# An encoder layer in fp32: input projection in seven block products, values in 512-wide products, chains in a new order

## The chip, the cores and the metric

The kernel runs on one core of a Trainium2 chip. The metric is the device time of one launch in microseconds (us), the median of the runs. A profile is one execution, recorded by the hardware profiler.

## The reference, cut to what matters

One encoder layer with shared weights runs on two groups of tokens: 256 of a prompt and 1024 of a sample, 1280 in all, width 1024. All is fp32.

```python
h = rmsnorm(x, g_mix_pre)
z = h @ w_in                      # 1024 x 9216
rq, rk, rv, rg, pin, mq, gl = split(z)    # six of 1024 columns, gl of 3072
gates  = sigmoid(gl)
y_ret  = retention_branch(rq, rk, rv, rg) @ w_ret_out   # rotary on q and k, chunks, both directions; silu(rg)
y_pool = pool_branch(pin) @ w_pool_out                  # moving means of width 2, 4, 8, 16
y_mem  = memory_branch(mq, mem) @ w_mem_out             # kv = rmsnorm(mem) @ w_mem_kv; softmax attention
merged = gates[0] * y_ret + gates[1] * y_pool + gates[2] * y_mem
x = x + rmsnorm(merged @ w_o, g_mix_post)
x = x + rmsnorm(conv_ffn(rmsnorm(x), w_up, conv_w, conv_b, w_down), g_ffn_post)
```

## The kernel before, in words

**Numbers.** A number is held as a high and a low part in a rounded fp32 format. `hilo` (L138) makes them: ScalarE copies to the high part (L140), VectorE subtracts for the low part (L141). A product is three matmuls, `mm3` (L147): high by high, high by low, low by high (L148 to L150), added up in one PSUM bank.

**Tiles.** The normed tokens lie transposed in SBUF as `hT`, eight tiles of 128 features by 1280 tokens, high and low. A *unit* is a 128 by 1024 tile of weights. For a feature-major unit, `fm_groups` (L481) makes 128 output features for three groups of tokens (512, 512, 256), with the weights as the stationary operand: 24 matmuls a group. For values, tokens are stationary and 256 columns of weights move, 24 matmuls for each 128 tokens (L624 to L630).

**Weights.** The class `Weights` (L59) takes units from one list `srcs` in the order of their use. A unit is loaded by SP into one of two raw tiles (L71), split by ScalarE (L87) and VectorE (L88) into one of four pairs of tiles, and taken by `take` (L96). The load of the unit after next is issued when a split is written.

**Order.** The program's order is written out by hand, and each engine runs its own instructions in that order. `tick` (L271) is called after each group of tokens (in the rotary units after each two groups): it splits a unit, issues one step of the weight sums, and takes one step of every chain in `bg`. A *chain* is a generator that does the work of one branch between `yield`s, beside the projections. The stages are:

1. The memory stage (L436 to L478): the statistics of mem and x, `hT`, the decay tables (`decay_tables` L398, with the decay matrix `dtab` and its load of `rel`), the memory's keys (8 units) and its values (4 heads, 256 columns each, L460 to L477), beside the chains `mem_stats`, `x_stats` and `decay_tables`.
2. Memory queries `mq` (8 units, VectorE copies them out of PSUM to SBUF, L619), then retention values (L622 to L635), beside `mem_chain` (L502): scores, softmax, products with the memory's values, stores of `om`.
3. Four times two pool units (`pool_unit`, L709) and a rotary query unit pair (`rotary_unit`, L726), then four key pairs, beside `pool_chain` (L645).
4. Retention gates `rg` (8 units, L826 to L834), beside `state_chain` (L750), which builds the states of the retention.
5. Branch gates (24 units, `gate_unit` L956). Beside the first of them runs `ret_chain` (L837): for each of 20 jobs (4 heads, 5 chunks) the scores, the products with values and with states, the norm, transposes and the store of `yr` (L934). It takes two steps a job and two steps a unit, after the groups of 512.
6. From 1347 us: products of the branches with their output weights, the output projection, the up projection, the convolution, the down projection.

**The up projection** (L1341 to L1555) makes two units (one gate, one value) of 1024 sample tokens with seven block products where eight would be direct. Four blocks of `h2` and three of their sums are kept (`hterm`), and two sums of weights a pair are made ahead, in DRAM, by DMAs: `sums` (L243) issues for each pair two plain DMAs on SP's queue (L251, L252) and four that accumulate on POOL's queue (L254 to L260), one step a tick, from the start of stage 2 on.

**Banks.** PSUM has eight banks of 512 columns: four for projections (`mmb`) and four for chains (`chb`).

Of the kernel before, what the change touches and what calls it, by code (L numbers as in the profile page):

```python
# [24 lines left out]
H = 4  # L25
# [13 lines left out]
PCOLS = PW - 2 * PAD  # L39
SLOT = 2 * T  # L40
# [18 lines left out]
class Weights:  # L59
# [8 lines left out]
    def load(self):  # L68
        if self.n_load < self.load_limit and self.n_load < self.n_split + self.RAW:
            t = self.pool.tile([P, 1024], F32, tag="wr", name="wr", bufs=self.RAW)  # L70
            self.nc.sync.dma_start(out=t, in_=self.srcs[self.n_load])  # L71
            self.raw[self.n_load] = t
            self.n_load += 1
# [22 lines left out]
    def take(self, n=1):  # L96
# [7 lines left out]
        return out  # L104

# [5 lines left out]
def encoder(ctx: ExitStack, tc: tile.TileContext, a: dict):  # L111
# [68 lines left out]
    w_in = a["w_in"]  # L180
    srcs = [a["w_kv"][i] for i in range(16)]
    srcs += [w_in[40 + i] for i in range(8)]
    srcs += [w_in[16 + i] for i in range(8)]
    for h in range(H):
        srcs += [w_in[32 + 2 * h], w_in[33 + 2 * h], w_in[2 * h], w_in[2 * h + 1]]
    srcs += [w_in[8 + i] for i in range(8)]
    srcs += [w_in[24 + i] for i in range(8)]
    srcs += [w_in[48 + i] for i in range(24)]
# [4 lines left out]
    s12_d = [dram.tile([P, 2, 512], F32, name=f"s12d{q}") for q in range(NF)]  # L193
    s34_d = [dram.tile([P, 2, 512], F32, name=f"s34d{q}") for q in range(NF)]
# [4 lines left out]
    for nm, q in stream:  # L199
        srcs.append({"u0": a["w_up"][q], "a2": a["w_up"][NF + q],  # L200
                     "s12": s12_d[q][:].rearrange("p a b -> p (a b)"),
                     "s34": s34_d[q][:].rearrange("p a b -> p (a b)")}[nm])
# [24 lines left out]
    vm_d = [dram.tile([P, 4, HD], F32, name=f"vm{h}") for h in range(H)]  # L227
    q_d = [dram.tile([P, NCH, 2, C], F32, name=f"qd{h}") for h in range(H)]
    k_d = [dram.tile([P, NCH, 2, C], F32, name=f"kd{h}") for h in range(H)]
    v_d = [dram.tile([P, NCH, 2, HD], F32, name=f"vd{h}") for h in range(H)]  # L230
# [12 lines left out]
    def sums():  # L243
        lag = 2

        def stage(i, q):
            u, v = (a["w_up"][n].rearrange("p (a b) -> p a b", b=512) for n in (q, NF + q))
            both = lambda x: x.unsqueeze(1).to_broadcast([P, 2, 512])
            s12, s34 = s12_d[q], s34_d[q]
            if i == 0:  # L250
                nc.sync.dma_start(out=s12[:], in_=both(v[:, 0, :]))  # L251
                nc.sync.dma_start(out=s34[:], in_=u)  # L252
            elif i == 1:
                nc.gpsimd.dma_start(out=s12[:], in_=both(v[:, 1, :]), accum_op=ALU.add)  # L254
            elif i == 2:
                nc.gpsimd.dma_start(out=s34[:, 0, :], in_=v[:, 0, :], accum_op=ALU.add)
            elif i == 3:
                nc.gpsimd.dma_start(out=s12[:, 1, :], in_=u[:, 0, :], accum_op=ALU.add)
            else:
                nc.gpsimd.dma_start(out=s34[:, 1, :], in_=s12[:, 1, :], accum_op=ALU.add)  # L260

        for n in range(NF + 4 * lag):
            for i in range(5):
                q = n - lag * i
                if 0 <= q < NF:
                    stage(i, q)
                    yield

    summing = [None]

    def tick(step=True):  # L271
        ws.tick()
        if summing[0] is not None:
            next(summing[0], None)
# [13 lines left out]
    ds = ExitStack()  # L288
    dec = ds.enter_context(tc.tile_pool(name="dec", bufs=1))
# [62 lines left out]
    def x_stats():  # L352
# [15 lines left out]
        xrb = s0.tile([P, T], F32, name="xrb")  # L368
# [27 lines left out]
    dtab = dec.tile([P, H, 2, C], F32, name="dtab")  # L396

    def decay_tables():  # L398
# [24 lines left out]
        nc.vector.tensor_scalar(out=kd, in0=kd, scalar1=HD ** -0.5, scalar2=None, op0=ALU.mult)  # L423
        yield
        rel = s0.tile([P, 2, 2 * C], F32, name="rel")
# [600 lines left out]
    for _ in summing[0]:  # L1026
        pass
# [734 lines left out]
```

## Time and profile before

| | |
|---|---|
| median of 3 runs | 2675.5 us (2675.26 to 2675.93) |
| the profiled execution's own time | 2674.43 us |
| span of the profile | 2672.7 us |
| TensorE busy | 2641.5 us, 14396 matmuls |
| VectorE, ScalarE, POOL busy | 1351.4, 919.5, 280.0 us |
| TensorE's granted clock, mean | 0.995 |

The span reaches from the first instruction to the last. A matmul's row covers its whole passage, so rows of neighbours overlap, and the busy time of TensorE says that it had work, not that it ran at its peak. Times in rows are us, and ns for the mean of one instruction. In a wait, the name behind the arrow is what ended it.

### The profile page before, as it was taken

The numbers are of one execution on the slowest core, as the hardware profiler recorded it, in microseconds if no ns is written. First come the engines' busy times: TensorE is split into PE (matmuls) and PEld (weight loads), VectorE is DVE, ScalarE is ACT, GpSimd is POOL, SyncE is SP. The second block draws the span as 40 slices with busy tenths as digits, with TensorE's granted clock in tenths as the row PEclk, the third lists the DMA queues.
The fourth block names the chain that finished last, engine by engine and source line by source line (L and its number), as shares of the span: only waits on it lengthen the run. The fifth ranks groups of instructions, "written<-read, shape, count | busy, mean of one in ns | idle before, by whom it ended". The sixth has DMA issues, their size and how long they took to land.

```text
span 2672.7 us, 36264 instructions
## 1 busy us (share of the span) xinstructions
PE 2641.5 (99%) x14396; PEld 2292.0 (86%) x14396; DVE 1351.4 (51%) x2267; ACT 919.5 (34%) x1567; POOL 280.0 (10%) x457
## 2 busy tenths in 40 slices
PE   8999999999999999999999999999999999999998
PEld 6999998888888888888888888877888888888887
DVE  5645303445445355555433453557666665664554
ACT  5433311221024332332312020565444444444443
POOL 1111221211123111111100000110000000000000
PEclk9999999999999999999999999998999999999999
DMA  7775565665477544444434353452333333354443
GB/s 263 255 197 142 142 154 158 149 170 142 123 177 215 170 155 150 142 156 147 141 133 138 107 168 97 146 185 92 113 109 116 111 111 110 116 190 148 140 159 111
DMA packets 145434, 397.57 MB, mean 149 GB/s; under 512 B 17680, under 2 KB 27792, under 8 KB 144912
## 3 DMA queue, kind: packets, MB, share of 16 engines
q1 hardware_dynamic: 100128, 267.02, 30.6%
q0 software_dynamic: 44848, 127.95, 17.6%
q8 instruction: 113, 1.85, 0.3%
q14 instruction: 57, 0.47, 0.1%
q10 hardware_dynamic: 288, 0.28, 0.0%
HBM read 303.69 MB, written 143.39 MB: 167 GB/s over the span
## 4 chain that ended last, share of the span: by engine, by line
PE 93%; issue 2%; DMA 2%; DVE 1%; ACT 1%; POOL 0%; SPq 0%; DVEq 0%; ACTq 0%; POOLq 0%
PE f L1316 15%; PE mm L149 13%; PE mm L148 13%; PE mm L150 13%; PE f L150 10%; PE f L149 10%; PE f L148 10%; PE ch L149 3%; PE ch L150 3%; PE ch L148 3%; DMA wr<-w_kv_in 0%; PE ch L559 0%; PE ch L931 0%; PE ch L769 0%; DMA x2d<-x 0%
## 5 line engine op out<-in xcount | busy, mean ns | idle before, releaser
L148 PE MATMUL mm<-b,wh 128*128 128x512 f32 (+1 forms) x1536 | 545.7, 355 | 0.0
L149 PE MATMUL mm<-b,wh 128*128 128x512 f32 (+1 forms) x1536 | 544.3, 354 | 0.0
L150 PE MATMUL mm<-b,wl 128*128 128x512 f32 (+1 forms) x1536 | 543.7, 354 | 0.0
L88 DVE TENSOR_TENSOR wl<-wr,wh 128x1024 fp32r<-128x1024 f32 x244 | 297.7, 1224 | 407.1 <-ACT wh L87 402.3
L87 ACT ACTIVATE wh<-wr 128x1024 fp32r<-128x1024 f32 x244 | 255.3, 1050 | 277.3 <-PE f L149 150.4
L150 PEld LDWEIGHTS mm<-b,wl 128*128 128x128 f32 x1536 | 290.0, 189 | 40.8
L148 PEld LDWEIGHTS mm<-b,wh 128*128 128x128 f32 x1536 | 290.4, 189 | 39.2
L149 PEld LDWEIGHTS mm<-b,wh 128*128 128x128 f32 x1536 | 290.4, 189 | 38.4
L1316 PE MATMUL f<-b,wh 128*128 128x512 f32 x880 | 274.3, 393 | 0.0
L1316 PEld LDWEIGHTS f<-b,wh 128*128 128x128 f32 x880 | 162.3, 190 | 30.7
L1316 PE MATMUL f<-b,wl 128*128 128x512 f32 x440 | 171.9, 391 | 0.0
L149 PE MATMUL f<-b,wh 128*128 128x512 f32 (+1 forms) x432 | 153.4, 355 | 0.0
L148 PE MATMUL f<-b,wh 128*128 128x512 f32 (+1 forms) x432 | 153.1, 355 | 0.0
L150 PE MATMUL f<-b,wl 128*128 128x512 f32 (+1 forms) x432 | 152.8, 354 | 0.0
L150 PE MATMUL f<-wh,gl 128*128 128x512 f32 x390 | 151.8, 389 | 0.1
L148 PE MATMUL f<-wh,gl 128*128 128x512 f32 x390 | 151.9, 389 | 0.0
L149 PE MATMUL f<-wl,gl 128*128 128x512 f32 x390 | 151.7, 389 | 0.0
L141 DVE TENSOR_TENSOR gl<-b,gl 128x640 fp32r<-128x640 f32 x78 | 64.4, 825 | 118.1 <-ACT gl L140 118.1
L964 ACT ACTIVATE gate<-mm 128x512 f32<-128x512 f32 (+1 forms) x68 | 35.5, 522 | 223.7 <-PE mm L150 133.0
L140 ACT ACTIVATE gl<-b 128x640 fp32r<-128x640 f32 x78 | 57.5, 740 | 153.9 <-PE f L150 153.9
L1316 PE MATMUL f<-hc,wh 128*128 128x512 f32 x352 | 108.9, 391 | 0.0
L148 PE MATMUL f<-h2p,wh 128*128 128x256 f32 x352 | 100.3, 285 | 3.3 <-ACT h2p L140 3.3
(343 smaller groups left out, 5293.5 us busy)
## 6 DMA issues: line engine op xcount, KB each, us to landing
wr<-w_in_in SPq DMA_DIRECT2D x72, 512.0 KB, 4.0
wr<-w_up_in SPq DMA_DIRECT2D x44, 512.0 KB, 3.6
wr<-w_down_in SPq DMA_DIRECT2D x44, 512.0 KB, 3.6
b<-fgd SPq DMA_DIRECT2D x44, 320.0 KB, 5.2
h2s<-gtd SPq DMA_DIRECT2D x48, 256.0 KB, 3.8
s12d<-w_up_in SPq DMA_DIRECT2D x22, 512.0 KB, 6.7
s34d<-w_up_in SPq DMA_DIRECT2D x22, 512.0 KB, 7.4
s12d<-w_up_in POOLq DMA_DIRECT2D x22, 512.0 KB, 7.8
```

The source lines that it names most:

```text
L87: self.nc.scalar.activation(h, r[:], AF.Copy)
L88: self.nc.vector.tensor_tensor(out=l, in0=r[:], in1=h.bitcast(F32), op=ALU.subtract)
L140: nc.scalar.activation(hi, src, AF.Copy)
L141: nc.vector.tensor_tensor(out=lo, in0=src, in1=hi.bitcast(F32), op=ALU.subtract)
L148: nc.tensor.matmul(out, ah, bh, start=first, stop=False)
L149: nc.tensor.matmul(out, ah, bl, start=False, stop=False)
L150: nc.tensor.matmul(out, al, bh, start=False, stop=last)
L964: nc.scalar.activation(y[:, 0:n], b, AF.Sigmoid)
L1316: nc.tensor.matmul(b, w[x][:, ks], hterm(nm, c, y), start=first and c == k == 0, stop=last and c == 3 and k == 2, skip_group_check=True)
```

## The change

- **Twelve pairs.** The units of `mq`, `pin` and `rg` are taken in twelve pairs. For a pair, the sample's 1024 tokens are made with seven block products (84 matmuls of 512) and the prompt's 256 tokens directly (48 of 256). Results go to DRAM (`mq_d`, `pin_d`, `g_d`), and the chains load them from there. The sums of tokens `T1` to `T4` are made by `in_terms` beside the values: xT is loaded again on ScalarE's queue, and VectorE and ScalarE scale, mix and split it.
- **Weight sums.** `sums` covers 34 pairs, twelve of the input projection ahead of the 22 of the up projection. Its first step goes to ScalarE's queue. Its steps start with the memory's values (one a tick), go on at two a tick in the values, and at one a released unit in the pairs (four a pair).
- **Values.** Both kinds are made 512 columns wide (`token_major`): four units are held for a half of the columns, and blocks of four token tiles fill four banks. ScalarE copies them out and stores them on its own queue, through two staging tiles (retention) or three (memory).
- **Order.** Memory keys; memory values; retention values; pairs; then keys beside `mem_chain` and one gate; nine gates beside `pool_chain` and `decay_matrix`; queries beside `state_chain`; gates beside `ret_chain`, which steps four times a unit, once of it in the middle of the first group; then the gates that are left. `rotary_unit` ticks after every group.
- `decay_matrix` (the load of `rel` and `dtab`) leaves the memory stage. In `ret_chain` the next job's split stands before the transposes and the output. Several pools wait tile by tile for the space that they reuse.

```diff
+    quads = [(k, i, w_in[o + 2 * i], w_in[o + 2 * i + 1])
+             for k, o in (("mq", 40), ("pin", 32), ("rg", 24)) for i in range(H)]
+    sum_rows = [q[2:] for q in quads] + [(a["w_up"][q], a["w_up"][NF + q]) for q in range(NF)]
...
             if i == 0:
-                nc.sync.dma_start(out=s12[:], in_=both(v[:, 0, :]))
-                nc.sync.dma_start(out=s34[:], in_=u)
+                nc.scalar.dma_start(out=s12[:], in_=both(v[:, 0, :]))
+                nc.scalar.dma_start(out=s34[:], in_=u)
...
+    N_MEM, N_POOL = 1, 9
     srcs = [a["w_kv"][i] for i in range(16)]
-    srcs += [w_in[40 + i] for i in range(8)]
     srcs += [w_in[16 + i] for i in range(8)]
...
+    for q in range(NQ):
+        srcs += [quad_srcs(nm, q, 0) for nm in ("u0", "s12", "s34", "a2")]
+    gates = [w_in[48 + i] for i in range(24)]
+    srcs += [w_in[8 + i] for i in range(8)] + gates[:N_MEM + N_POOL]
+    srcs += [w_in[i] for i in range(8)] + gates[N_MEM + N_POOL:]
...
+    def token_major(base, lhs, nt, out):
+        blocks = [range(4)] if nt == 4 else [range(4), (4,), (5,), range(6, nt)]
+        for p in range(2):
+            ids = [base + 4 * p + i for i in range(4)]
+            for g, ts in enumerate(blocks):
+                bs = {t: (mmb if len(ts) > 1 else chb)(512) for t in ts}
+                for i, u in enumerate(ids):
+                    wh, wl = ws.hold(u)
+                    for t in ts:
+                        for c in range(2):
+                            k, cs, cols = 2 * i + c, slice(t * P, (t + 1) * P), slice(c * 512, (c + 1) * 512)
+                            mm3(bs[t], lhs[k][:, 0, cs], lhs[k][:, 1, cs], wh[:, cols], wl[:, cols],
+                                k == 0, k == KC - 1)
+                        if i == 3:
+                            out(p, t, bs[t])
+                    if g == len(blocks) - 1:
+                        ws.free(u)
+                    if len(ts) > 1 or i == 3:
+                        tick()
...
+        def v_out(p, t, b):
+            o = vp.tile([P, 512], F32, tag="vst", name="vst", bufs=2)
+            nc.scalar.activation(o, b, AF.Copy)
+            nc.scalar.dma_start(out=v_d[p][:, t], in_=o[:].rearrange("p (a b) -> p a b", b=HD))
+
+        bg.append(in_terms(vp))
+        adding[0] = 2
+        token_major(v_at, hT, NT, v_out)
...
+        for q in range(NQ):
+            d, more = Q[q], q + 1 < NQ
+            product(d["a"], unit("s12", q, 1), "T2", False, True)
+            u2 = snap(qtile("u2", 2)[:], d["a"])
+            pr(q, 0, 1)
+            d["d"] = mmb(512)
+            product(d["d"], unit("s34", q, 0), "T3", True, True)
+            product(d["a"], unit("s12", q, 0), "T1", False, True)
+            u4 = snap(qtile("u4", 1)[:], d["a"])
+            release("s12", q)
+            pr(q, 1, 1)
+            close(q, 1, TP + HS, minus, d["d"], u4)
+            if more:
+                p1(q + 1)
+            product(d["a"], unit("s34", q, 1), "B22", False, True)
+            emit(q, 0, TP + HS, HS, d["a"])
+            release("s34", q)
+            if more:
+                pr(q + 1, 0, 0)
+            product(d["d"], unit("a2", q, 1), "T4", False, True)
+            close(q, 1, TP, minus, d["d"], u2)
+            release("a2", q)
+            if more:
+                pr(q + 1, 1, 0)
+                p2(q + 1)
...
+    bg.append(mem_chain())
+    cs_ = rotary_consts(mp)
+    for h in range(H):
+        rotary_unit(k_d[h], mp, *cs_)
+    for _ in range(N_MEM):
+        gate_unit(mp)
...
+    bg.append(pool_chain())
+    bg.append(decay_matrix(pp))
+    for _ in range(N_POOL):
+        gate_unit(pp)
...
+        bg.append(state_chain(rp))
+        cs_ = rotary_consts(rp)
+        for h in range(H):
+            rotary_unit(q_d[h], rp, *cs_)
+        while bg:
+            gate_unit(rp)
...
+            split(n + 1)
             if n:
                 transp(n - 1)
+            load(n + 2)
             output(n)
-            split(n + 1)
-            load(n + 2)
...
+        bg.append(ret_chain(rp))
+        while bg and gate_n[0] < 23:
+            gate_unit(rp, stepped)
+        drain()
```

In `emit`, a result of `mq` or `pin` is copied by ScalarE where it is not yet in SBUF, one of `rg` goes through a sigmoid (ScalarE) and a product (VectorE) with a second tile; all of these share five tiles of 128x512, and POOL stores them.

## Rows read from the trace of the kernel before

**Rows 1.** The page, part 1: busy time, share and instructions of each engine.
```profile
PE 2641.5 (99%) x14396; PEld 2292.0 (86%) x14396; DVE 1351.4 (51%) x2267; ACT 919.5 (34%) x1567; POOL 280.0 (10%) x457
```

**Rows 2.** The page, part 4: the chain that ended last, by engine.
```profile
PE 93%; issue 2%; DMA 2%; DVE 1%; ACT 1%; POOL 0%; SPq 0%; DVEq 0%; ACTq 0%; POOLq 0%
```

**Rows 3.** Windows by stage: PE, PEld, DVE, ACT, POOL busy; clock; DMA share; GB/s.
```profile
59.00:113.00 54.00, 49.92 (x396) 49.50 (x395) 39.16 (x45) 27.52 (x36) 10.26 (x19) 0.94 0.74 263
113.00:270.00 157.00, 157.00 (x967) 141.21 (x966) 75.19 (x143) 54.36 (x121) 24.69 (x29) 1.00 0.66 179
...
676.00:786.00 110.00, 110.00 (x588) 95.42 (x587) 48.88 (x77) 13.48 (x15) 21.39 (x30) 1.00 0.58 148
786.00:932.00 146.00, 146.00 (x812) 126.95 (x811) 66.48 (x119) 59.52 (x129) 39.23 (x62) 1.00 0.69 195
932.00:1316.00 384.00, 384.00 (x2231) 339.32 (x2230) 212.45 (x571) 116.92 (x200) 46.75 (x80) 1.00 0.44 146
```

**Rows 4.** The chain in order of time, two successive pairs' starts: start, us, what.
```profile
1871.78 5.47 PE f L1316 x24
...
1896.65 5.47 PE f L1316 x24
```

**Rows 5.** Windows inside the values and the up projection; columns as in rows 3.
```profile
340.00:400.00 60.00, 60.00 (x503) 60.00 (x502) 4.72 (x4) 10.03 (x15) 13.09 (x18) 1.00 0.67 164
...
1910.00:2010.00 100.00, 100.00 (x533) 86.53 (x533) 60.61 (x68) 43.37 (x57) 4.33 (x8) 1.00 0.34 112
```

**Rows 6.** Waits between 59 and 113 us: total us, times, longest us.
```profile
ACT wh L87 <- DMA wr<-w_kv_in: 4.3, 3, 2.9
...
PE mm L149 <- DVE wl L88: 2.3, 1, 2.3
...
PE mm L148 <- ACT wh L87: 1.8, 1, 1.8
```

**Rows 7.** Timeline of VectorE and of ScalarE, 44 to 46 us: start, us, instruction.
```profile
44.16 0.49 DVE L429 TENSOR_SCALAR dtab<-rel,lg 128x512 f32<-128x512 f32 x1 [3.22 <-DMA rel<-rel_in]
...
45.47 0.63 ACT L432 ACTIVATE dtab<-dtab 128x512 f32<-128x512 f32 x1 [4.84 <-DVE dtab L430]
```

**Rows 8.** DMA issues, value stores: count, KB each, median us to landing.
```profile
vd<-vst POOLq DMA_DIRECT2D x20, 256.0 KB, 2.4
```

**Rows 9.** Window with the sums' first steps; columns as in rows 3.
```profile
120.00:140.00 20.00, 20.00 (x112) 17.44 (x111) 5.55 (x8) 3.81 (x4) 3.27 (x4) 1.00 0.96 293
```

**Rows 10.** Lines L251 and L256: ns of an issue; L256's us to landing.
```profile
L251 SPq DMA_DIRECT2D s12d<-w_up_in x22: 547/553/674, 120.7 to 686.7; - x22
...
L256 POOL DMA_DIRECT2D s34d<-w_up_in x22: 886/920/2014, 139.5 to 824.1; - x22
...
DMA to landing us min/median/max: 4.3/6.3/17.8
```

**Rows 11.** VectorE's groups, 935 to 1316 us: busy, mean ns, idle before.
```profile
L88 DVE TENSOR_TENSOR wl<-wr,wh 128x1024 fp32r<-128x1024 f32 x21 | 25.7, 1225 | 71.5 <-ACT wh L87 71.5
L912 DVE SCALAR_TENSOR_TENSOR y<-ch,qdec,y 128x256 f32<-128x256 f32 x48 | 23.2, 484 | 34.0 <-PE ch L150 33.4
...
L141 DVE TENSOR_TENSOR sthl<-str,sthl 128x512 fp32r<-128x512 f32 x20 | 13.9, 693 | 15.1 <-ACT sthl L140 15.1
L933 DVE TENSOR_TENSOR yo<-ch,gr 128x512 f32<-128x512 f32 x20 | 13.8, 692 | 34.9 <-PE ch L931 34.9
```

**Rows 12.** Line L933, outputs of the retention: ns min/median/max, first and last start.
```profile
L933 DVE TENSOR_TENSOR yo<-ch,gr x20: 691/692/693, 958.7 to 1315.9; 128x512 f32<-128x512 f32 x20
```

**Rows 13.** TensorE's timeline at 1802 us, and a window behind it.
```profile
1802.61 0.66 PE L1142 MATMUL f<-ident,x 128*128 128x128 f32 x4 [1.25 <-ACT x L1135]
1805.19 1.11 PE L1142 MATMUL f<-ident,x 128*128 128x128 f32 x4 [1.93 <-ACT h2s L1152]
...
1806.00:1810.00 4.00, 4.00 (x12) 3.13 (x11) 2.35 (x5) 3.38 (x10) 0.96 (x2) 0.50 0.44 131
```

More of the change, by code (lines that the diff above doesn't have):

```diff
@@ L39 @@
 PCOLS = PW - 2 * PAD
+PWA = 1408
 SLOT = 2 * T
@@ L104, in take, with hold, free @@
         return out
+    def hold(self, i):
+        while self.n_split <= i:
+            assert self.can_split()
+            self.split()
+        return self.hl[i]
+    def free(self, i):
+        self.hl.pop(i)
+        self.n_taken += 1
+        self.n_done += 1
+        self.split()
     def can_split(self):
@@ L241, in encoder, with sum_step @@
     bg = []
[L243 to L250, printed above, removed]
-                nc.sync.dma_start(out=s12[:], in_=both(v[:, 0, :]))
-                nc.sync.dma_start(out=s34[:], in_=u)
[L253 to L269, printed above, removed]
+    def sum_step(n=1):
+        for _ in range(n):
+            next(summing, None)
+    adding = [0]
     def tick(step=True):
         ws.tick()
-        if summing[0] is not None:
-            next(summing[0], None)
+        sum_step(adding[0])
         for g in list(bg) if step else ():
@@ L484, in fm_groups @@
             for c in range(KC):
+                if mid and o == 0 and c == KC // 2:
+                    mid()
                 cs = slice(c * P, (c + 1) * P)
@@ L576, in mem_chain @@
         load_k(0)
+        load_q(0)
+        load_q(1)
         load_v(0)
-        for _ in range(4):
-            yield
+        yield
+        yield
+        yield
         split_k(0)
-        split_v(0)
-        while 0 not in mq:
-            yield
         split_q(0)
         yield
+        split_v(0)
         n = len(jobs)
@@ new lines, in encoder, with gate_out, gate_unit @@
+    gate_n = [0]
+    def gate_out(m, pool, o, n, b):
+        y = pool.tile([P, 512], F32, tag="gate", name="gate", bufs=3) if pool else stile(n)
+        nc.scalar.activation(y[:, 0:n], b, AF.Sigmoid)
+        nc.gpsimd.dma_start(out=gate_d[m][:, o:o + n], in_=y[:, 0:n])
+    def gate_unit(pool, mid=None):
+        m = gate_n[0]
+        gate_n[0] += 1
+        (wh, wl), = ws.take()
+        for o, n, b in fm_groups(wh, wl, hT, mid=mid):
+            gate_out(m, pool, o, n, b)
+            tick()
@@ L610, in encoder, with stepped @@
+    def stepped():
+        for g in list(bg):
+            try:
+                next(g)
+            except StopIteration:
+                bg.remove(g)
     bg.append(mem_chain())
-    summing[0] = sums()
+    cs_ = rotary_consts(mp)
     for h in range(H):
-        while h >= 2 and h - 2 not in mq_done:
-            tick()
-        t = mp.tile([P, 2, T], F32, tag="mq", name="mq", bufs=2)
-        for e in range(2):
-            (wh, wl), = ws.take()
-            for o, n, b in fm_groups(wh, wl, hT):
-                nc.vector.tensor_copy(t[:, e, o:o + n], b)
-                if e == 1 and o == GROUPS[-1][0]:
-                    mq[h] = t
-                tick()
@@ L812, in state_chain @@
         load(1)
-        for _ in range(4):
-            yield
+        yield
+        yield
         for n in range(len(jobs) + 1):
@@ L954, in ret_chain @@
         transp(len(jobs) - 1)
[L956 to L974 removed]
+    with tc.tile_pool(name="rtp", bufs=1, reuse_waits="tile") as rp:
+        bg.append(ret_chain(rp))
+        while bg and gate_n[0] < 23:
+            gate_unit(rp, stepped)
+        drain()
     ds.close()
```

423 lines of the change are left out of this document (251 added, 172 removed).

## The prediction

> **What bounds the kernel now.** I read the page's busy times first: TensorE is busy 99% of the span, no other engine above 51% [rows 1]. The chain of waits agrees: 93% of it is TensorE, DMA has 2% [rows 2]. A share can hide stages with another limit, so the windows by stage come next: in each window shown between 113 us and 1316 us TensorE is busy in every microsecond at a granted clock of 1.00, while VectorE fills a third to a bit over a half and the DMA engines 44 to 69% [rows 3]. The memory stage alone (59 to 113 us) loses time. So between 113 and 1347 us, where the change sits, the time is the number of matmuls times the time of each, as long as nothing new makes TensorE wait. A profile's busy matmul row overlaps its neighbours, so the pace is taken from repetition. In the up projection, which already uses seven block products, 24 matmuls of 512 columns follow each other in 5.47 us, that is 0.228 us each, and from the same place of one pair to that of the next, a pair of units takes 1896.65 - 1871.78 = 24.87 us [rows 4]. In the value projection 503 matmuls of 256 columns touch a 60 us window [rows 5]; less two cut by its edges, 0.12 us each.
>
> **What is removed.** A unit (128 output features, 1280 tokens) is 24 x (2 x 0.228 + 0.12) = 13.8 us, a pair 27.6 us. The seven products are 84 matmuls of 512 and the prompt keeps 48 of 256: 84 x 0.228 + 48 x 0.12 = 24.9 us, which is what rows 4 show for such a pair. Twelve pairs save 144 matmuls of 512, **32.8 us**. Values go from 960 matmuls of 256 (115.2 us) to 480 of 512 (109.4 us): **5.8 us**. The memory's values go from 384 of 256 (46.1 us) to 192 of 512 (43.8 us): **2.3 us**. Chains, keys, queries and gates keep their matmuls. Sum: 40.9 us.
>
> The Trainium skill (TensorE: Matmul & The Clock Gate, Back-to-back issue gap) gives N/2.4 + 2.5 ns for one matmul, 215.8 ns at 512 columns and 109.2 at 256. By it the three terms would be 31.1, 1.2 and 0.5 us, 32.8 in all; the row of this kernel at 256 columns, 120 ns, decides.
>
> **What is added beside TensorE.** Each needs a cover, and each is bounded.
>
> *Decay matrix moved out of the memory stage.* Its loads and three VectorE steps a head held VectorE and then ScalarE's weight split (ScalarE idle 4.84 us, VectorE 3.22 us, waiting for it and its DMA) [rows 7]. TensorE later waited 1.8 and 2.3 us for split weights [rows 6]. Gain 0 to 4.1 us; I take 1, because a weight load waited for its DMA there too [rows 6].
>
> *Sums earlier.* Forty-eight of their steps are now issued before the first pair: 8 in the memory stage, beside the loads of x, and 40 in the value stage, two a tick where it was one. The first step's two DMAs go from SP's queue to ScalarE's, where value stores and new loads of xT also go; four accumulating DMAs stay on POOL. The two issues take 0.55 us each on SP's sequencer [rows 10], 1.1 us per set on ScalarE, which is 34% busy [rows 1]: nothing. Where sums were issued fastest so far, the DMA engines were 96% busy [rows 9], and one accumulation took up to 17.8 us to land against a median of 6.3 [rows 10]; the memory stage already had 74% [rows 3]. The weights are needed one unit per 5.5 us there. Cost 0 to 12 us; I take 2: the ring of four split units covers a late load of some 15 us, and the projected tokens use hT one chunk pair at a time, later than the old first unit.
>
> *Value stores.* Four banks of 512 finish together at the end of each half, with two staging tiles, so the third copy waits until the first store has landed. A store landed in 2.4 us [rows 8], but now shares a queue with the sums. TensorE wants the third bank 2.7 us after the half ends. With 2.4 us there is no wait; with a landing like the accumulations' upper end about 7 us, twice. Queued behind that copy on ScalarE are weight splits, with several ticks of slack, and the first pair's snapshot. 0 to 14 us; I take 2.
>
> *Extra splits and evictions in the pairs.* Four units a pair are split instead of two, and three snapshots and three differences are added. The up projection carries the same load and more at TensorE 100 of 100 us, VectorE 61, ScalarE 43 [rows 5]. What differs: outputs leave on POOL's queue behind accumulations, through five tiles (gates of the retention use two tiles an output). 0 to 12 us (1 us a pair); I take 0, because a bank is wanted again only two pairs later.
>
> *Chains beside keys and queries.* Keys and queries cost VectorE 48.9 us per 8 units with their splits [rows 3], 6.1 a unit, 4.9 without the split. The memory chain's stage had VectorE at 75.2 of 157 us [rows 3], 48%; 4.9 us per unit-with-chain period (157 us over about 6.6 units, 23.7 us) makes 69%. The state chain's stage had 46% [rows 3]; 4.9 per 18.3 us makes 72%. No engine fills, but a chain step behind a 256-column group now sits behind rotary work. 0 to 11 us (1.4 us in each of 8 unit pairs); I take 1. The pool chain runs beside nine gates, which leave VectorE to it: 0.
>
> *Retention at double pace.* Before, one job per gate unit: 20 outputs from 958.7 to 1315.9 us [rows 12], 18.8 us apart, that is 13.8 us of gate and 5.0 us of the job's own matmuls. Now four steps a unit (one inside the first group), so two jobs: 6.9 + 5.0 = 11.9 us. VectorE needs (212.5 - 25.7) / 20 = 9.3 us a job and half a split, 9.9 us [rows 3, 11]: 83%. It fits, but chunks with both states need more than the mean and steps are unevenly spaced. 0 to 10 us (half a us a job); I take 3, above the other stages since the cover is thinnest here. Fewer gates stay beside this chain; the rest moved to the pool, so their sum is unchanged.
>
> **Sum.** -40.9 - 1 + 2 + 2 + 0 + 1 + 3 = -33.9 us. The profiled execution took 2674.43 us, span 2672.7; the median of the runs is 2675.5, 1.07 above. 2674.43 - 33.9 + 1.07 = 2641.6, say **2641 us**. All covers complete and the full gain of the memory stage: 2675.5 - 45.0 = 2630.5.
>
> **Rivals.**
> *The DMA engines crowd the start.* For it: 96% busy [rows 9] with half the pace of sums. Against it: that was with several first steps in one burst, and weights still arrived. At the upper ends (12 and 14 us in place of 2 and 2) it gives 2641 + 22 = 2663 us. Chance 0.2. The Trainium skill (Trainium Kernel Development and Optimization, Key Constraints) says that DMAs of all queues share the same 16 engines and another queue saves only issue time; by that, moving the first step to ScalarE's queue buys no room, and rows 9 agree that the engines were the limit.
>
> *Retention becomes VectorE's, and the kernel slower.* In the old stage VectorE stood 34.0, 34.9 and 15.1 us waiting for TensorE's products, its transposes and ScalarE [rows 11], 84 us over 20 jobs, 4.2 a job. If those waits are the job's own latency and not slack, a job takes 9.9 + 4.2 = 14.1 us, not 11.9: 44 us over 20 jobs in place of my 3, 2641 + 41 = 2682 us, slower than before. It decides from (2675.5 - 2641) / 20 = 1.7 us a job above my allowance. Against it: at half the pace TensorE came late by design, so most of those waits are slack. Chance 0.07; with half of it, 2661, another 0.05.
>
> *TensorE's clock.* After pauses of 1.25 and 1.93 us between transposes the granted clock was 0.50 for 4 us, 1.2 in place of 2.4 GHz, and 12 matmuls stood in a 4 us window [rows 13]. A boundary that pauses that long costs 2 us on top: two such, 2645. Chance 0.05, inside my range.
>
> *The seven products hold TensorE up, so that a pair takes its old 27.6 us.* Then 32.8 us are lost again: 2674, no change. Against it are the 24.87 us of rows 4. Chance 0.03.
>
> **How the numbers follow.** Forecast with its bounds, 2630 to 2652: 0.6. Crowding 0.2, half the retention rival 0.05, clock 0.05: up to 2663 and all faster. No change 0.03 and 0.02 of mishaps at the edges: same 0.05. Slower 0.07. Faster 0.88 (they leave 0.6 + 0.2 + 0.05 + 0.05 less the 0.02). 0.2% is 5.4 us, about what a measurement of this kernel can tell from no change. Range **2630 to 2664**.
>
> **What would show it.** Right: TensorE busy without gaps from the values to the last gate; a pair every 24.9 us; 480 and 192 fewer matmuls for values and 144 fewer for pairs; retention outputs about 11.9 us apart; values at 0.228 us a matmul. Wrong: ScalarE waiting for a value store or VectorE for xT with TensorE idle behind it; outputs of the retention over 13 us apart with VectorE above 90%; split weights late in the memory stage; a clock under 1.00 at a stage's start.

## The result, and the profile after

The changed kernel takes **2715.4 us** (median of 4 runs, 2714.7 to 2716.4), the kernel before 2675.4 us in the same session (4 runs): ratio 1.015, 95% interval 1.0132 to 1.0167. The change costs 40 us where 34 us of gain were forecast. The profiled execution took 2714.7 us, its span 2712.9.

The page of the changed kernel, parts 1 and 4:

```profile
PE 2622.4 (97%) x13580; PEld 2240.8 (83%) x13580; DVE 1415.7 (52%) x2343; ACT 982.7 (36%) x1637; POOL 335.4 (12%) x525
...
PE 83%; DMA 6%; DVE 5%; ACT 3%; issue 2%; POOL 0%; SPq 0%; ACTq 0%; DVEq 0%; POOLq 0%
```

The matmuls did go: 816 fewer records than in [rows 1], 144 + 480 + 192. But in the chain that ended last TensorE's share fell from 93% [rows 2] to 83%, and DMA, VectorE and ScalarE hold 14% in place of 4%. Windows of the changed kernel by stage (columns as in [rows 3]): memory from 60 us, values, pairs, keys, pool, queries, retention.

```profile
60.00:117.00 57.00, 49.30 (x202) 39.51 (x200) 39.28 (x44) 24.36 (x24) 11.89 (x17) 0.91 0.96 318
117.00:252.00 135.00, 114.13 (x481) 92.67 (x482) 41.47 (x49) 30.93 (x46) 25.26 (x28) 0.92 0.98 254
252.00:551.00 299.00, 298.45 (x1584) 257.75 (x1583) 95.60 (x106) 92.57 (x134) 74.09 (x108) 1.00 0.75 211
551.00:753.00 202.00, 199.03 (x1237) 179.95 (x1236) 121.08 (x232) 73.85 (x164) 45.73 (x60) 0.99 0.76 208
753.00:945.00 192.00, 162.54 (x791) 136.75 (x790) 77.39 (x90) 61.63 (x85) 51.35 (x98) 0.90 0.69 183
945.00:1090.00 145.00, 144.03 (x787) 124.10 (x786) 87.50 (x159) 45.78 (x102) 35.86 (x53) 1.00 0.76 207
1090.00:1388.00 298.00, 297.19 (x1786) 264.20 (x1784) 217.90 (x590) 110.59 (x191) 36.08 (x61) 1.00 0.54 184
```

Three rows stand out by an idle TensorE and a clock well under 1.00: the memory stage, the values and the pool. Before, the two windows that hold the values and the pool had neither:

```profile
270.00:405.00 135.00, 135.00 (x1129) 135.00 (x1129) 26.57 (x48) 34.24 (x66) 29.97 (x41) 1.00 0.59 148
405.00:676.00 271.00, 271.00 (x1398) 232.51 (x1397) 128.34 (x167) 56.54 (x86) 49.53 (x91) 1.00 0.58 152
```

In the value row of the changed kernel the DMA engines are at 0.98 and VectorE at 41.5 of 135 us. In the pool row nothing is full: VectorE is busy for 77 of 192 us, and TensorE stands still for 29.

To price the stages I use one measure throughout, **the time over pace**: the distances between the starts of successive matmul rows, less 0.228 us for 512 columns, 0.120 for 256 and at most 0.108 for 128, added up from the stage's first matmul to the next stage's (the pool's from its first product on). It holds waits, slower matmuls at a lower clock and missing records alike. The value stage as a check: 480 matmuls of 0.228 us are 109.4 us, and the window has 135.0.

| over pace, us | before | after | difference |
|---|---|---|---|
| memory stage and what is ahead of it | 18.7 | 25.4 | +6.7 |
| values | 0.0 | 25.4 | +25.4 |
| pairs (before: `mq` units) | -0.1 | 0.3 | +0.4 |
| keys with the memory chain (before: memory chain) | 2.0 | 7.4 | +5.4 |
| pool (before: pool, queries, keys) | -0.5 | 40.1 | +40.6 |
| queries with the state chain (before: state chain) | 1.4 | 3.4 | +2.0 |
| retention | 2.8 | 5.0 | +2.2 |
| the rest | 20.1 | 18.1 | -2.0 |

The differences add up to 80.7 us; less the 40.9 us of matmuls that went, the kernel should be 39.8 us slower, and it is 40.0. That the sum closes follows from the measure, which takes the paces as given. That the removed matmuls were paid out is shown by a stage that runs at its pace: the pairs are 0.3 us over it, and the values 2.2 us in the run without the pairs' weight sums (below). Stalls took twice as much back, nearly all in two places.

**The pool.** What TensorE waited for from 745 to 960 us (total us, times, longest):

```profile
PE ch L162 <- ACT dh L154: 23.6, 5, 7.7
PE ch L163 <- DVE dh L155: 5.0, 5, 1.2
PE ch L162 <- ACT ypo L975: 0.9, 1, 0.9
```

And ScalarE in the same stretch:

```profile
ACT dh L154 <- DVE ps L959: 44.5, 8, 8.9
ACT ypo L975 <- DMA ypd<-ypo: 42.8, 8, 6.3
```

`dh` is the split input of the pool's product with its weights. TensorE waits for its high part, ScalarE for the sums `ps` that VectorE makes first. VectorE's timeline for the two tiles of the group of width 4 (of the second only the last step stands here), and TensorE's beside it:

```profile
813.03 1.23 DVE L90 TENSOR_TENSOR wl<-wr,wh 128x1024 fp32r<-128x1024 f32 x1 [9.37 <-ACT wh L89]
...
814.77 1.52 DVE L939 TENSOR_TENSOR ps<-pin 128x1310 f32<-128x1310 f32 x1
816.33 1.52 DVE L944 TENSOR_TENSOR ps<-ps 128x1308 f32<-128x1308 f32 x1
...
818.29 1.51 DVE L959 SCALAR_TENSOR_TENSOR ps<-ps,pin 128x1296 f32<-128x1296 f32 x1
821.15 1.51 DVE L155 TENSOR_TENSOR dh<-ps,dh 128x1296 fp32r<-128x1296 f32 x1 [1.35 <-ACT dh L154]
...
828.94 1.51 DVE L155 TENSOR_TENSOR dh<-ps,dh 128x1296 fp32r<-128x1296 f32 x1 [1.35 <-ACT dh L154]
```

```profile
821.17 0.58 PE L162 MATMUL ch<-dh,pwh 128*128 128x256 f32 x1 [5.14 <-ACT dh L154]
...
828.96 0.58 PE L162 MATMUL ch<-dh,pwh 128*128 128x256 f32 x1 [5.46 <-ACT dh L154]
```

A group's two tiles go through VectorE from 814.8 to 830.5 us, one instruction after the other, and TensorE stands for 5.1 us before the first tile's product and for 5.5 us before the second's. VectorE had been idle for 9.4 us until 813.0: it had room, but its next instruction was the low part of a weight split, and ScalarE was late with the high part:

```profile
810.88 0.69 ACT L975 ACTIVATE ypo<-ch,pk 128x512 f32<-128x512 f32 x1 [5.03 <-DMA ypd<-ypo]
...
811.94 1.06 ACT L89 ACTIVATE wh<-wr 128x1024 fp32r<-128x1024 f32 x1
```

ScalarE stood there for the stores of the group before. So two things make this group late: its sums begin late, behind a weight split that waits for those stores, and they stand close before their use. No tile was missing: all eight of ScalarE's waits for `dh` end with VectorE's sums. TensorE's waits are 29.5 us of the 40; the clock, 0.90 in this stage, slows the matmuls between them.

**The start.** TensorE's waits from 60 to 252 us, then three of ScalarE's:

```profile
PE mm L162 <- ACT vst L615: 15.3, 3, 13.2
PE mm L162 <- ACT st L522: 13.3, 4, 5.4
```

```profile
ACT T L154 <- DVE xs L557: 36.4, 8, 18.9
ACT vst L615 <- DMA vd<-vst: 22.0, 6, 5.6
ACT st L522 <- DMA vm<-st: 12.9, 2, 6.9
```

DMAs issued from 117 to 252 us (count, KB each, median us to landing):

```profile
vd<-vst ACTq DMA_DIRECT2D x18, 256.0 KB, 6.4
s12d<-w_in_in POOLq DMA_DIRECT2D x8, 512.0 KB, 11.5
xs<-xT_in ACTq DMA_DIRECT2D x8, 512.0 KB, 9.2
```

A value store that took 2.4 us before [rows 8] takes 6.4. ScalarE's timeline around the longest wait shows the order in which it pays for that:

```profile
184.93 1.06 ACT L89 ACTIVATE wh<-wr 128x1024 fp32r<-128x1024 f32 x1 [6.11 <-DMA wr<-w_in_in]
...
189.07 0.63 ACT L154 ACTIVATE T<-xs 128x512 fp32r<-128x512 f32 x1 [3.09 <-DVE xs L557]
191.06 0.63 ACT L154 ACTIVATE T<-xs 128x512 fp32r<-128x512 f32 x1 [1.36 <-DVE xs L557]
191.59 0.58 ACT L615 ACTIVATE vst<-mm 128x512 f32<-128x512 f32 x1
```

The bank that TensorE had wanted for 13.2 us is copied out behind a weight split and two splits of token terms. The weight split waited 6.1 us for its load; the terms wait for VectorE, whose own half of that weight split stands ahead of them. At the stage's first copies it was the other transfer: ScalarE stood 18.9 us for terms whose tokens had not landed.

**As forecast:** two pairs' same place in the chain, and the retention's outputs.

```profile
290.30 5.47 PE mm L639 x24
...
315.18 5.47 PE mm L639 x24
```

```profile
L1163 DVE TENSOR_TENSOR yo<-ch,gr x20: 680/684/692, 1125.1 to 1349.4; 128x512 f32<-128x512 f32 x20
```

A pair takes 24.88 us, and twenty outputs come (1349.4 - 1125.1) / 19 = 11.8 us apart.

### The profile page after: what moved, and what is told of

It is laid out like the page before. It is cut to its first block, busy times and chain, and to the rows that moved or that the text cites. A ratio compares the mean times of both kernels' runs of the same rounds, so it can differ in the third digit from the quotient of the medians.

```text
span 2712.9 us, 35194 instructions
## 1 busy us (share of the span) xinstructions
PE 2622.4 (97%) x13580; PEld 2240.8 (83%) x13580; DVE 1415.7 (52%) x2343; ACT 982.7 (36%) x1637; POOL 335.4 (12%) x525
## 3 DMA queue, kind: packets, MB, share of 16 engines
q1 hardware_dynamic: 111072, 268.33, 29.5%
## 4 chain that ended last, share of the span: by engine, by line
PE 83%; DMA 6%; DVE 5%; ACT 3%; issue 2%; POOL 0%; SPq 0%; ACTq 0%; DVEq 0%; POOLq 0%
PE f L1521 15%; PE f L164 10%; PE f L163 10%; PE f L162 10%; PE mm L639 7%; PE mm L162 6%; PE mm L163 6%; PE mm L164 6%; PE ch L163 3%; PE ch L164 3%; PE ch L162 3%; PE ch L639 1%; DMA wr<-w_kv_in 1%; DMA vm<-st 1%; DMA vd<-vst 1%
## 5 line engine op out<-in xcount | busy, mean ns | idle before, releaser
L90 DVE TENSOR_TENSOR wl<-wr,wh 128x1024 fp32r<-128x1024 f32 x268 | 327.5, 1224 | 516.1 <-ACT wh L89 511.2
L89 ACT ACTIVATE wh<-wr 128x1024 fp32r<-128x1024 f32 x268 | 280.7, 1051 | 269.1 <-PE f L163 150.6
L162 PE MATMUL mm<-b,wh 128*128 128x512 f32 (+1 forms) x960 | 342.6, 357 | 0.0
L163 PE MATMUL mm<-b,wh 128*128 128x512 f32 (+1 forms) x960 | 341.1, 355 | 0.0
L164 PE MATMUL mm<-b,wl 128*128 128x512 f32 (+1 forms) x960 | 340.5, 355 | 0.0
L164 PEld LDWEIGHTS mm<-b,wl 128*128 128x128 f32 x960 | 182.2, 190 | 25.7
L162 PEld LDWEIGHTS mm<-b,wh 128*128 128x128 f32 x960 | 182.5, 190 | 24.2
L163 PEld LDWEIGHTS mm<-b,wh 128*128 128x128 f32 x960 | 182.5, 190 | 23.6
L639 PE MATMUL mm<-T,wh 128*128 128x512 f32 x384 | 118.9, 391 | 0.5 <-ACT q L568 0.5
```

What stands on the lines that cost most here:

```text
L89: self.nc.scalar.activation(h, r[:], AF.Copy)
L90: self.nc.vector.tensor_tensor(out=l, in0=r[:], in1=h.bitcast(F32), op=ALU.subtract)
L162: nc.tensor.matmul(out, ah, bh, start=first, stop=False)
L163: nc.tensor.matmul(out, ah, bl, start=False, stop=False)
L164: nc.tensor.matmul(out, al, bh, start=False, stop=last)
L639: nc.tensor.matmul(b, w[x][:, ks], in_term(nm, c, y), start=first and c == k == 0, stop=last and c == 3 and k == 2, skip_group_check=True)
```

## The experiments

Each is an edit of the changed kernel (2715.4 us). Where no number of runs stands, the time is one execution. Five kernels with the same start have 25 to 31 us over pace in the values, and the kernels with the same pool 36 to 41 in the pool, so 5 us or less is not read from a single execution.

**The pool: more staging.** The pool's outputs get six staging tiles instead of two, so that ScalarE does not stand at their stores.

```diff
-                    y = pp.tile([P, 512], F32, tag="ypo", name="ypo", bufs=2)
+                    y = pp.tile([P, 512], F32, tag="ypo", name="ypo", bufs=6)
```

> Six staging tiles for the pool branch's outputs in place of two. Theory (ScalarE is held by those stores: it waited 42.8 us in eight waits for one of two tiles to land, and the pool's own high parts, the gates' evictions and weight splits stand behind it): these waits go to under 5 us, TensorE's waits for dh between 745 and 960 us fall from 28.6 us to under 12 (the first group, whose loads come late at the stage's start, keeps some 9), and the time falls by 20 to 28 us. Rival (the pool's VectorE work or its late loads don't fit beside nine gates): ScalarE's waits go over to other causes and the time falls by under 8 us.

Measured: 2707.6 us, pool 28.1 us over pace. ScalarE's 42.8 us of waiting for stores are gone, but TensorE's waits keep their form (745 to 960 us):

```profile
PE ch L162 <- ACT dh L154: 13.6, 3, 7.7
PE ch L163 <- DVE dh L155: 4.4, 4, 1.2
```

So the stores held up a part, 8 us of the time and 12 us in the pool, and most of the loss has another cause.

**The pool: no weight sums beside it.** They stop for the stage and are caught up beside the queries.

```diff
     bg.append(pool_chain())
+    adding[0] = 0
...
+        adding[0] = 2
```

> No step of the sums is issued beside the nine gates and the pool chain; two a tick follow beside the queries. Theory (the pool stores land late because they follow accumulations on POOL's queue and share the engines with the first step): ScalarE's waits for them fall from 42.8 us to under 20, and the time by 10 to 20 us. Rival (with two tiles for three evictions in a row even an undisturbed landing of 2.3 us holds ScalarE, or the stage's late start counts): under 6 us.

Measured: 2718.0 us. The DMA share of the stage falls from 0.69 to 0.41 and the pool to 30.4 us over pace, but the queries rise to 9.8 and the retention to 8.2. The gain is given back later. In the pool it is 10 us, about what the six tiles gave, and it goes with the same stores. ScalarE's 42.8 us of waiting for them are down to

```profile
ACT ypo L975 <- DMA ypd<-ypo: 10.4, 6, 3.0
```

The other 30 us stay with the DMA engines at 0.41: crowding is not what the pool waits for there.

**The pool: the decay matrix beside the queries**, with the six staging tiles.

```diff
-    bg.append(decay_matrix(pp))
...
+        bg.append(decay_matrix(rp))
```

> Six tiles for the pool branch's outputs, and the decay matrix beside the queries in place of the pool chain. With six tiles alone TensorE's excess over its pace in the pool stage fell from 40 to 28 us and the time from 2714.7 to 2707.6 us. If the decay matrix (its load, four exponentials with table loads of ScalarE, twelve VectorE steps) holds up the pool's first group, that group's stall of 7.8 us goes and the time falls to 2696 to 2702 us. If the pool chain's own order is too short (a group's second high and low parts are written two steps ahead of their use, about 14 us, and take VectorE some 16 to 22 us a group), the first group keeps its stall or most of it, the second and fourth keep 4 us each, and the time stays over 2703 us.

Measured: 2706.5 us; pool 22.2, with 1.9 more just ahead of its first product, queries 8.0 (from 3.4). Against the six tiles alone, less work on VectorE helps the pool by 4 us, no more than the scatter, and costs 5 beside the queries. The chain alone still stalls TensorE.

**The pool: the chain one group ahead.** The pool's amount of work is the same. The sums and splits of group g are now written before the products of group g - 1, whose two halves stand one gate group apart; there are three `dh` tiles, two of `pwh` and three of `ypo`, and the decay matrix stands beside the queries.

```diff
-        for g, w in enumerate(WINDOWS):
+        for g, w in enumerate(WINDOWS + (0,)):
...
+                if g and c == 0:
+                    output(g - 1, 0)
+                    yield
+                    output(g - 1, 1)
+                    yield
```

> The pool chain is written one group ahead: a group's two outputs follow the next group's first preparation, with three tiles for high and low parts in place of two, three tiles for outputs, one step more for the loads, and the decay matrix beside the queries. The instructions of the pool are the same. Theory (the cover between a preparation and its use is what fails in the pool stage, not the amount of VectorE's work): TensorE's excess in that stage goes from 40 to under 8 us and the time to 2676 to 2690 us. Rival (nine gates are not enough for the stage's work or its loads, whatever the order): the excess stays over 20 us and the time over 2695 us.

Measured: **2677.5 us**, pool 0.4 us over pace. The stage's window (columns as in [rows 3]):

```profile
753.00:912.00 159.00, 159.00 (x823) 136.39 (x822) 72.09 (x81) 48.37 (x72) 49.60 (x90) 1.00 0.87 237
```

TensorE is without a gap at a clock of 1.00, while VectorE and the DMA engines are no emptier than before. ScalarE even waits for pool stores again (745 to 960 us), and TensorE does not feel it:

```profile
ACT ypo L937 <- DMA ypd<-ypo: 16.0, 8, 7.6
```

37.9 us come back. Not all of it is order, since the decay matrix has left the stage and there are more tiles. But the run before had the late decay matrix and more staging, and still 24 us over pace in the pool: these 24 us come back by the order and the tiles that it needs. So the step that decided was not how full VectorE was but how far ahead of its use its work was written.

**The start: no weight sums for the pairs.**

```diff
-        for n in range(len(sum_rows) + 4 * lag):
+        for n in range(NQ, len(sum_rows) + 4 * lag):
...
+        if not at:
+            return sum_rows[q][0 if nm in ("u0", "s12") else 1]
...
-        adding[0] = 1
...
-        adding[0] = 2
```

> The weight sums of the twelve pairs are left out, the pairs read plain rows of weights of the same size in their place, and the sums of the up projection start with the pairs at one step a released unit. Theory (the sums crowd the DMA engines, 96 and 98% busy in the memory and value stages, so xT, weights and value stores land late and ScalarE's order holds the evictions behind them): from 60 us to the first pair 192 us become 160 to 168, the time falls by 24 to 31 us. Rival (two staging tiles and the second load of xT are enough for it): under 10 us.

Measured: 2691.8 us, 23.7 less, just under the theory's range; memory stage 21.7, values 2.2 us over pace. DMAs from 117 to 252 us:

```profile
xs<-xT_in ACTq DMA_DIRECT2D x8, 512.0 KB, 4.0
...
vd<-vst ACTq DMA_DIRECT2D x20, 256.0 KB, 2.0
```

With the sums gone, stores and token tiles land in a third to a half of the time, and the value stage runs at its pace. The sums' traffic is the cause; the rest of this group asks by which way it reaches TensorE.

**The start: the sums' first step back on SP's queue.**

```diff
-                nc.scalar.dma_start(out=s12[:], in_=both(v[:, 0, :]))
-                nc.scalar.dma_start(out=s34[:], in_=u)
+                nc.sync.dma_start(out=s12[:], in_=both(v[:, 0, :]))
+                nc.sync.dma_start(out=s34[:], in_=u)
```

> The two DMAs of the sums' first step go back to SP's queue, nothing else. Theory (all queues share the DMA engines, only the amount counts): the time stays within 5 us, value stores land in about 6 us as before. Rival (value stores and xT stand behind the first step in ScalarE's queue): value stores land in under 4 us and the time falls by over 10 us.

Measured: 2712.6 us, values 28.4: no difference that a single execution can tell, and none of the 10 us of the rival. The Trainium skill (Trainium Kernel Development and Optimization, Key Constraints) says that the queues share 16 DMA engines and another queue saves issue time alone; this run agrees (2712.6 against 2715.4 us).

**The start: fewer sums, but not in the first half.** None in the memory stage, one a tick in the second half of the values, five a pair.

```diff
-        adding[0] = 1
         token_major(8, memT, 4, mem_v)
...
+            if p == 0 and t == NT - 1:
+                adding[0] = 1
...
-            sum_step()
+            sum_step(2 if nm == "u0" else 1)
```

> No sums beside the memory's values; two steps a tick in the first half of the values, one in the second, five a pair in place of four in the pairs: some 35 steps ahead of the first pair, not 48. Theory (amount of DMA work ahead of the pairs): the 51 us of excess in the memory and value stages fall by 10 to 20 us, half to two thirds of what leaving the sums out gave (23 us), and the time to 2695 to 2706 us. Rival (any sums beside the second load of xT are too much): under 6 us. The pairs keep 24.9 us each by the theory; if the sums' last steps come late there, they lose 1 us or more each.

Measured: 2711.9 us; memory stage 21.7, values 27.8. The longest wait for a value copy is still 18.3 us, at the middle of the values. The same edit on top of the pool chain one group ahead:

> The pool chain one group ahead and the sums spread, together. If the two losses are separate, the gains add: 2660 to 2678 us, at or below the kernel before (2674.4). If the spread sums only move the crowding into the pool stage, the sum of the gains is not reached and the time stays over 2685 us.

Measured: 2675.8 us (before on the same chip 2674.6), values 26.6. That is in the range, but by the pool alone, which gave 2677.5. Fewer sums in the second half buy nothing.

**The start: two sets of banks in turn.** A block of four never needs the banks that the block before it filled.

```diff
-                bs = {t: (mmb if len(ts) > 1 else chb)(512) for t in ts}
+                bs = {t: (chb if (p if nt == 4 else g) else mmb)(512) for t in ts}
```

> The changed kernel with one line other: the four accumulators of a block of four in the value projection, and of the memory's values, come from the two sets of PSUM banks in turn, so that a block of four never needs the banks that the four tokens just before it filled. The DMA traffic is the same. Changed kernel: 2714.7 us; TensorE over its pace by 25 us in the memory stage and by 25 us in the value stage. Theory (the crowded DMA engines only make the evictions late, and TensorE pays because it needs these four banks again at once; the longest single wait is 13 to 18 us at the middle of the values): the value stage falls to under 12 us over, and the time to 2698 to 2704. Rival (the crowding holds up TensorE itself in any case, by weights or token tiles that land late, and the wait goes to the next full set of banks): the value stage stays over 20 us and the time over 2709.

Measured: 2718.0 us. The memory stage falls by 11 us to 14.2, and the values rise to 40.7. TensorE's waits from 60 to 252 us:

```profile
PE ch L162 <- ACT vst L615: 27.8, 2, 16.3
PE mm L162 <- ACT wh L89: 5.2, 1, 5.2
```

The wait went to the next block of four. The copies are late by more than the slack that four banks give, so the banks are not the cause; the rival holds.

**The start: the token terms' high parts on VectorE**, so that ScalarE does not stand behind late token tiles.

```diff
-            hilo(r, in_term(nm, c, 0), in_term(nm, c, 1))
+            nc.vector.tensor_copy(in_term(nm, c, 0), r)
+            nc.vector.tensor_tensor(out=in_term(nm, c, 1), in0=r, in1=in_term(nm, c, 0).bitcast(F32),
+                                    op=ALU.subtract)
```

> The changed kernel with the high parts of the four combined token terms written by VectorE instead of ScalarE (16 tiles of 512 columns), so that ScalarE, which evicts the values, no longer stands in its order behind tiles that wait for token rows still on their way. The evictions still wait for their two staging tiles. In the changed kernel ScalarE waited 36 us for VectorE's terms and 22 us for value stores in the two stages, and TensorE was over its pace by 25 us in the value stage. Theory (the evictions are late because ScalarE stands behind the terms): the value stage falls to under 13 us over, the time to 2700 to 2705. Rival (they are late because the value stores land in 6 us and more, with two staging tiles): the value stage stays over 18 us, the time over 2708.

Measured: 2708.0 us, values 21.9; between the two. ScalarE's largest wait from 60 to 252 us is now

```profile
ACT vst L617 <- DMA vd<-vst: 44.7, 7, 11.9
```

The 36.4 us behind the terms went, and the waits for stores doubled from 22.0 us. Each of the two late transfers holds ScalarE up; with one gone, the other takes most of its place.

**The start: half the sums in the values.** One a tick in both halves instead of two, and five a pair.

```diff
-        adding[0] = 2
         token_major(v_at, hT, NT, v_out)
...
-            sum_step()
+            sum_step(2 if nm == "u0" else 1)
```

> The changed kernel with one weight sum per tick in the value stage instead of two (20 steps of the sums there instead of 40, 10 instead of 20 in its first half), as before one per tick in the memory's values, and five per pair instead of four, which makes up for them. Unlike the run that spread the sums, which kept 20 in the first half of the values, this one thins out just that half, where TensorE's long wait for the value evictions arises. Theory (the value stores land late because the sums in the first half fill the DMA engines): the value stage falls from 25 to under 14 us over, the time to 2701 to 2706. Rival (the second load of the tokens and the weights fill the engines there, and half as many sums do not open them): the value stage stays over 20 us, the time over 2709.

Measured: 2704.5 us, values 16.2. The time is in the theory's range, the stage 2 us above its bound. DMAs from 117 to 252 us:

```profile
vd<-vst ACTq DMA_DIRECT2D x20, 256.0 KB, 3.2
xs<-xT_in ACTq DMA_DIRECT2D x8, 512.0 KB, 7.7
```

Stores land in half the time at the median, and the stage loses 9 us less. Against the run with the spread sums, which had 20 of them in the first half, this one has 10 there: it is the first half of the values, with the second load of the tokens, that has no room. The tokens' load keeps a share: the stage is still 14 us above the run without sums.

**All together.** First the pool chain ahead with the two sets of banks:

> The pool chain written one group ahead (as in the run of that name, 2677.5 us) and the two sets of banks in turn, both on the changed kernel. If the two losses are separate, their gains add: 37 us of the pool, and what the run with the banks alone gains. Theory of the banks: 2658 to 2669 us, 6 to 16 us under the kernel before. Rival of the banks: 2672 to 2678 us, no difference from the kernel before.

Measured: 2683.3 us (7 runs), ratio to before 1.0029, interval 1.0017 to 1.0040; values 40.9. It is above both ranges: the banks alone cost the values more than they save. Then the terms on VectorE as well:

> The same term tiles on VectorE, with the pool chain one group ahead and the two sets of banks in turn (2683.3 us without the terms' move, TensorE over its pace by 41 us in the value stage). Theory (evictions behind the terms): the value stage falls by 20 us or more, the time to 2655 to 2664, under the kernel before by 0.4% or more. Rival (stores and staging tiles): over 2675.

Measured: 2675.3 us (10 runs), ratio 1.0001, interval 0.9992 to 1.0011; values 32.7. The move gives 8 us, not 20; the rival's stores hold the rest. Last, half the sums too:

> The same thinner sums in the kernel with the pool chain one group ahead, two sets of banks in turn and the terms on VectorE (2675.3 us; TensorE over its pace by 33 us in the value stage). Theory: the value stage falls by 12 us or more, the time to 2655 to 2664, 0.4% or more under the kernel before. Rival: 2671 to 2678, no difference from before.

Measured: **2665.2 us** (5 runs, 2658.9 to 2668.0) against 2674.2 for before, ratio 0.9958, interval 0.9944 to 0.9972. It misses the theory's range by 1 us and is faster than both kernels. In the profiled execution (2668.0 us) its value and pool stages (columns as in [rows 3]):

```profile
104.00:240.00 136.00, 118.18 (x485) 95.42 (x484) 61.50 (x75) 29.86 (x37) 21.70 (x24) 0.91 0.89 239
...
741.00:905.00 164.00, 162.72 (x837) 139.08 (x836) 75.01 (x84) 49.16 (x73) 51.32 (x98) 1.00 0.85 234
```

The value stage is still 25.9 us over pace. That is about what lies between this kernel and the forecast (24 us). Here half the sums did not bring the stores in earlier (issued from 117 to 252 us, DMA share 0.87):

```profile
vd<-vst ACTq DMA_DIRECT2D x20, 256.0 KB, 6.9
```

Together the banks and the terms' move show no gain. Memory and value stage together are 38.4 us over pace here and 40.3 with half the sums alone, and the pool's order and the thinner sums by themselves, 37.9 and 10.9 us, would make 2666.6 us of 2715.4, an estimate for a kernel that was not run.

## Why the prediction was wrong

**The step that failed is the pool chain.** "The pool chain runs beside nine gates, which leave VectorE to it: 0" cost 40.6 us. The prediction priced the chain by how full VectorE would be, and VectorE was indeed not full: 77 of 192 us. It never asked when in the program's order a group's sums stand against the products that use them. At width 4 the first tile's sums stand three ticks ahead, the second's two. A tick here is a gate group of 24 matmuls, 5.5 or 2.9 us, so that is 13.8 and 8.4 to 10.9 us of TensorE's work, against 15.7 us on VectorE for the two tiles (814.8 to 830.5 us). Before, the pool's products were spread over 231 us; now they stand within 159, stalls included:

```profile
L148 PE MATMUL ch<-dh,pwh x48: 280/392/395, 443.7 to 675.1; 128*128 128x512 f32 x32, 128*128 128x256 f32 x16
...
L162 PE MATMUL ch<-dh,pwh x48: 278/397/628, 772.4 to 930.9; 128*128 128x512 f32 x32, 128*128 128x256 f32 x16
```

Nor did it ask what holds ScalarE up in that stage, the stores behind two tiles. Step by step the runs took the 40 us apart: 12 went with more staging, 4 with the decay matrix moved (within the scatter), 24 with the order. No rival covered any of it. That the same work one group earlier costs the pool nothing is shown by the run with 0.4 us over pace.

**The start was sized too small.** The two terms "sums earlier" and "value stores" stood at 2 us each, with upper ends of 12 and 14; the memory and value stages lost 32 us. The rival "the DMA engines crowd the start" had the mechanism, and leaving out the sums returned 23.7 us. Two things were missed in it. The landing was taken from a stage with the sums alone (2.4 us for a store); beside twice the sums and the second load of the tokens it was 6.4, the accumulations' median [rows 10], which the term named only by its upper end and did not take. And "queued behind that copy are weight splits" looked at what waits behind the copy, not at what the copy waits behind: ScalarE had weight splits and term splits ahead of it, and these wait for weights and tokens. "Nothing" for the sums on ScalarE's queue was right: back on SP's queue nothing changed.

**Right:** the terms of removed matmuls as far as they can be seen at pace, the pairs (0.3 us over) and the values (2.2 over without the pairs' sums); the pairs at 24.9 us with 0.4 us more stalls than before, and with them the fall of the rival that they hold TensorE up; the retention at 11.8 us a job (11.9 forecast) and 2.2 us more over pace (3 forecast). A retention bound by VectorE, the one rival by which the kernel would be slower, did not come; the kernel is slower for another reason.

**Off by little:** chains beside keys and queries, 7.4 us where 1 was taken, inside the bounds of 0 to 11. The gain from moving the decay matrix can't be told apart inside the memory stage. The clock rival had the right sign, but it came as a part of the long waits: 0.90 to 0.92 in the three stages that stall, and 1.00 in the pool once its waits were gone. VectorE's shares were misread: the windows of [rows 3] from 113 us on give 44 to 55%, not a third to a bit over a half. No term hangs on it.

What stays open: how much of the 14 us that the values still lose with half the sums is the tokens' second load. That load was not left out in any run. Open too is whether more staging tiles for the value stores would help, as they did in the pool: ScalarE waits 22.0 us for these stores in the changed kernel and 48.1 in the last one, and no run has more than the two tiles. And why a store with half the sums lands in 3.2 us in one kernel and in 6.9 in the other is not shown.

## What to carry to other kernels

A chain beside a bound engine needs two figures: how full its engine is, and how far ahead of its use its work is written, against the time from its first instruction to its last. When a stage beside a chain gets shorter, that distance shrinks with it. For an eviction, list what stands ahead of it in its engine's order and which transfer each of these waits for; and when two late transfers meet on one engine, taking away one shows little until the traffic that delays both is thinned.

## What the hardware showed that was not expected

The stages with waits lost more than the waits: in the pool 29.5 us of waits went with 40 us over pace, at a mean clock of 0.90, and without waits the clock was 1.00. The time that a store of 256 KB took to land rose with the DMA share (117 to 252 us, medians): 2.0 us at 0.40 (no sums), 3.2 at 0.83 (half of them), 6.4 at 0.98. But the share alone does not set it: in the last kernel it was 6.9 us at 0.87.
